# The first microseconds of a four-layer decoder trunk: one DMA queue, tokens and first weights ahead, tap tables later, unread products on TensorE

## Chip, core and metric

One NeuronCore of a Trainium2 chip runs the whole program. The metric is device time in microseconds (us). In the profile PE is TensorE (matmuls and transposes), PEld its weight loads, DVE VectorE, ACT ScalarE, POOL GpSimd and SP SyncE; SPq and ACTq are the DMA queues that SyncE and ScalarE issue on.

## What is computed

The input is 256 tokens of width 1024. Four layers follow; layer i mixes tokens by a gated convolution (i = 0 and 3), a state-space scan (1) or differential attention (2), then attends to 256 memory tokens, then runs a SwiGLU. Each sub-layer ends in a layer norm of alpha * x + f(x). The change touches the start of the program and the convolution:

```python
def conformer_conv(x, w_in, b_in, w_dw, b_dw, ln_g, ln_b, w_out, b_out):
    h = x @ w_in + b_in                      # 1024 -> 2048
    a, gate = jnp.split(h, 2, axis=-1)
    h = a * jax.nn.sigmoid(gate)
    h = causal_depthwise_conv(h, w_dw, b_dw) # 31 taps
    h = jax.nn.silu(layer_norm(h, ln_g, ln_b))
    return h @ w_out + b_out

def reference(x, mem, ...):
    for i in range(4):
        y = (conformer_conv, ssd_mixer, diff_attention)[i % 3](x, ...)
        x = post_norm(x, y, ...)
        x = post_norm(x, memory_cross_attention(x, mem, ...), ...)
        x = post_norm(x, swiglu(x, ...), ...)
    return x
```

## The kernel before

Products of f32 numbers are made of three fp32r matmuls each: a number is split into a rounded high part and the rest (`split`: ScalarE copies the high part, VectorE subtracts), and `mm3` (L199 to L202) adds high x high, high x low and low x high in one PSUM bank.

Weights stream through `_Weights`. A block is 128 x 1024 numbers (512 KB). `_load` (L136 on) takes one of 4 raw buffers, issues the block's DMA (for `cv_w_in` two of 256 KB each, L145), then has ScalarE make the high part `wh` (L152) and VectorE the low part `wl` (L155) in a ring of 7. A raw buffer is free again when its `wl` is made. `get` first calls `prefetch`, which runs `_load` up to AHEAD = 3 blocks past the one wanted.

The tokens are held as two tiles x of 128 rows. `transpose_split` turns a tile on TensorE (L226, four 128x128 transposes into one of two "m" banks), then splits the result into XTh and XTl (L213, L215). The same function turns the memory tokens into MT.

`conv` runs `gated(c)` for four column groups of `w_in`. One `gated` takes four weight blocks and runs `gemm_a`: for t = 0 and 1, for k = 0 to 7, one `mm3` of 512 columns, so 48 matmuls, each block serving two k; after each t, `done` adds the bias (L544), gates (L545, L546), and after every second c splits the result (uh, ul; tiles ch and cl). The convolution is done with a 160-point Fourier transform held as a table `dft`: `front(t, c)` multiplies by the table (6 matmuls for t = 0, 12 for t = 1) and by the spectrum of the taps H on VectorE (L566 to L571), and splits; `rear(t, c)` transforms back (6 matmuls, which need that split). H itself is made in `conv_tables`: 8 f32 matmuls of 31 rows (L502), with a VectorE copy (L503) after each pair's half. Between the gated groups `kv_fill` runs key and value units of the memory attention.

The program order at the start: `conv_loads` (the two small loads ftap and taps on ScalarE's queue, into raw buffers), `setup` (tokens, first weight block, transposes), `conv_tables` (H), then `conv`: gated(0), `conv_dft` (the table, into a raw buffer), both memory tiles, gated(1), ... A planner orders the instructions of each engine by priority (program order, unless `high_priority` raises it) and its own estimate of when each is ready; each engine then runs its list strictly in order. `gemm_a` takes a dict `between`: work to be emitted after a given (t, k), whose TensorE instructions come behind that product (`behind`). Before, gated(2) emits front(0, 0) after (0, 5) and rear(0, 0) and front(1, 0) after (1, 3). Layer 3's convolution uses the same functions, with its loads and tables made during the SwiGLU of layer 2.

Of the kernel before, what the change touches and what calls it, by code (L numbers as in the profile page):

```python
# [9 lines left out]
F32 = mybir.dt.float32  # L10
F32R = mybir.dt.float32r
BF16 = mybir.dt.bfloat16
# [5 lines left out]
P = 128  # L18
# [70 lines left out]

class _FromRaw:  # L90


    def __init__(self, raw):
        self.raw = raw

    def tile(self, shape, dtype, tag, name):
        return self.raw.tile([P, D], dtype, tag="raw", name=name)[0 : shape[0], 0 : shape[1]]

# [11 lines left out]
class _Weights:  # L110
# [3 lines left out]
    def __init__(self, nc, ins, raw_pool, ring_pool, plan):  # L114
        self.nc, self.ins, self.raw_pool, self.ring_pool = nc, ins, raw_pool, ring_pool
        self.plan, self.record = plan, isinstance(nc, _Trace)
        self.pos = self.loaded = 0
        self.ready = {}

    def get(self, name, i, k0, nk, *segs):  # L120
        key = (name, i, k0, nk, segs)
        if self.record:
            self.plan.append(key)
            return self.nc, self.nc
        assert self.plan[self.pos] == key
        self.prefetch(min(len(self.plan), self.pos + 1 + AHEAD))
        wh, wl = self.ready.pop(self.pos)
        self.pos += 1
        return wh, wl
# [5 lines left out]

    def _load(self, q):  # L136
        nc = self.nc
        name, i, k0, nk, segs = self.plan[q]
        n = sum(c for _, c in segs)
        raw = self.raw_pool.tile([P, 1024], F32, tag="raw", name=f"raw{q}")[:, : nk * n]  # L140
        raw3 = raw.rearrange("p (k n) -> p k n", k=nk)
        src = self.ins[name][i]
        at = 0
        for c0, c in segs:
            nc.sync.dma_start(  # L145
                out=raw3[:, :, at : at + c],
                in_=src[k0 * P : (k0 + nk) * P, c0 : c0 + c].rearrange("(k p) n -> p k n", p=P),
            )
            at += c
        wh = self.ring_pool.tile([P, 1024], F32R, tag="wh", name=f"wh{q}")[:, : nk * n]  # L150
        wl = self.ring_pool.tile([P, 1024], F32R, tag="wl", name=f"wl{q}")[:, : nk * n]
        nc.scalar.copy(out=wh, in_=raw)  # L152
        m = nk * n // LO_PARTS
        for a in range(0, nk * n, m):
            nc.vector.tensor_tensor(  # L155
                out=wl[:, a : a + m], in0=raw[:, a : a + m], in1=wh[:, a : a + m].bitcast(F32), op=ALU.subtract
            )
        self.ready[q] = (
            wh.rearrange("p (k n) -> p k n", k=nk),
            wl.rearrange("p (k n) -> p k n", k=nk),  # L160
        )


class _Trunk:
# [45 lines left out]
    def split(self, src, dh, dl, scale=1.0):  # L210

        nc = self.nc
        nc.scalar.activation(out=dh, in_=src, func=AF.Copy, scale=scale)  # L213
        if scale == 1.0:
            nc.vector.tensor_tensor(out=dl, in0=src, in1=dh.bitcast(F32), op=ALU.subtract)  # L215
        else:
            nc.vector.scalar_tensor_tensor(
                out=dl, in0=src, scalar=scale, in1=dh.bitcast(F32), op0=ALU.mult, op1=ALU.subtract
            )

    def transpose_split(self, nat, dh, dl, t, halves=(0, 1)):
        nc = self.nc
        for j in halves:
            ps = self.bank("m", a=4)
            for i in range(4):
                nc.tensor.transpose(ps[:, i, :], nat[:, (4 * j + i) * P : (4 * j + i + 1) * P], self.ident)  # L226
            dst = (slice(None), slice(4 * j, 4 * j + 4), slice(t * P, (t + 1) * P))
            self.split(ps, dh[dst], dl[dst])

# [166 lines left out]

    def setup(self):
        nc, ins = self.nc, self.ins
# [16 lines left out]
        early = self.const.tile([P, 1], F32, name="early")  # L415
        nc.scalar.activation(out=early, in_=self.mhalf[:, 0:1], func=AF.Tanh)
        for t in range(T):
            for c in range(2):
                cs = slice(c * 512, (c + 1) * 512)
                nc.sync.dma_start(out=self.x[t][:, cs], in_=ins["x"][0][t * P : (t + 1) * P, cs])  # L420
            with self.tc.high_priority():
                self.transpose_split(self.x[t], self.XTh, self.XTl, t)
            if t == 0:
                self.W.prefetch(1)

    def load_mem(self):
        for t in range(T):
            m = self.raw.tile([P, D], F32, tag="raw", name=f"mem{t}")
            self.nc.sync.dma_start(out=m, in_=self.ins["mem"][0][t * P : (t + 1) * P, :])
            self.transpose_split(m, self.MTh, self.MTl, t)  # L430

# [52 lines left out]
    def conv_loads(self, pool, tmp, j):  # L484

        nc, ins = self.nc, self.ins
        ftap = tmp.tile([TAPS, 2 * NC], F32, tag="small", name=self.uid("ftap"))
        nc.scalar.dma_start(out=ftap, in_=ins["dft"][0:TAPS, 4 * NC : 6 * NC])
        taps = tmp.tile([TAPS, D], F32, tag="rows", name=self.uid("taps"))
        nc.scalar.dma_start(out=taps, in_=ins["cv_w_dw"][j])  # L490
        return {"raw": (ftap, taps)}

# [12 lines left out]
    def conv_dft(self, pool, tmp, j, pre):  # L505

        nc, ins = self.nc, self.ins
        dft = tmp.tile([P, DFT_COLS], F32, tag="rows", name=self.uid("dft"))
        nc.sync.dma_start(out=dft, in_=ins["dft"])
# [7 lines left out]
    def conv(self, i, j, pre):  # L517
# [5 lines left out]
        with self.stage_pool(f"cv{j}", 1) as pool, self.stage_pool(f"cw{j}", 2) as wk:  # L523
# [9 lines left out]
            def gated(c, between={}):  # L533
# [19 lines left out]

                self.gemm_a("cv_w_in", j, ((c * 256, 256), (D + c * 256, 256)), done, "i", between)

# [19 lines left out]
            def rear(t, c):  # L575
                self.mm3(nat[t][c], *back[0], *ysp, True, False)
                self.mm3(nat[t][c], *back[1], *psp, False, True)
                nc.vector.bn_stats(out=st[t][:, c, :], in_=nat[t][c])

            gated(0)  # L580
            if "late" in pre:
                pre.pop("late")()
            dfts, H, yre = pre["dft"], pre["H"], pre["yre"]
            now = [[d[:, q * NC : (q + 1) * NC] for d in dfts] for q in range(2)]
# [3 lines left out]
            psp = [pool.tile([NF, 512], F32R, name=f"cv_z{e}") for e in "hl"]  # L588
            if first:
                self.load_mem()  # L590
            gated(1)
            bo = self.bcast_row("raw", ins["cv_b_out"][j], self.raw)
            for t in range(T):
# [32 lines left out]
            fill = KV_CONV[j]  # L626
            gated(2, {(0, 5): lambda: front(0, 0), (1, 3): lambda: (rear(0, 0), front(1, 0))})
            self.kv_fill(i, fill[0])
# [767 lines left out]
    def run(self):  # L1396
        n = 0
        ctx = ExitStack()
        pre, (loads, tables, late) = self.prepare(0, ctx, _FromRaw(self.raw))
        loads()  # L1400
        self.setup()
        tables()
        pre["late"] = late
        for i in range(DEPTH):
# [67 lines left out]
```

## Time and profile before

| | us |
|---|---|
| median of 3 runs (lowest, highest) | 1749.15 (1746.3, 1751.69) |
| the profiled execution, its own time | 1747.02 |
| its span from first to last instruction | 1745.3 |

TensorE is busy 98% of the span. The first of the 40 slices of the page (43.6 us each) is the one in which it is least busy, with 6 tenths. Times below are microseconds from the start of the span unless marked ns. A start and a duration stand first in a timeline row; a bracket at its end says how long the engine was idle before it and what ended that. A pipelined matmul's duration overlaps the next one's, so the pace of a run of matmuls is read from start to start. "PEclk" in a table of stretches is the granted clock as a share of full speed (2.4 GHz; 0.5 is 1.2 GHz).

### The profile page before, as it was taken

To read this page: it belongs to the slowest core of one execution; us is meant where nothing else is said; L and a number is where in the kernel's file an instruction comes from. 1 tells how busy PE (TensorE), PEld (TensorE's weight loads), DVE (VectorE), ACT (ScalarE), POOL (GpSimd) and SP (SyncE) were. 2 spreads that over 40 slices of the span, in tenths; PEclk is the share of its full clock that TensorE was granted. 3 is DMA by queue.
4 is the path that set the end of the run, shared out by engine and by line. 5 is a ranking of instruction groups with operands and counts; after the bars stand their busy time and mean duration, and the time that the engine had idled before them with its cause. 6 is when DMAs were issued, how large, how long until landed. Compare 5 with 4: busy or idle time off the path is not lost.

```text
span 1745.3 us, 25786 instructions
## 1 busy us (share of the span) xinstructions
PE 1704.7 (98%) x9788; PEld 1470.4 (84%) x9788; DVE 1283.2 (74%) x1965; ACT 905.4 (52%) x1436; POOL 67.8 (4%) x72
## 2 busy tenths in 40 slices
PE   6999999999999999999999999999999999999998
PEld 4898888888999998888888888888788878878886
DVE  4898776668898778776668677776666888876666
ACT  3455555554665654455554565545454445645552
POOL 0000000000011110000000000000000000000000
PEclk9999999999999999999999999999999999999999
DMA  6656376666666545376665643647566645556662
GB/s 227 218 169 202 117 217 186 188 191 181 193 182 173 181 146 191 115 219 192 192 186 190 180 133 109 193 143 216 161 192 194 211 151 167 184 168 189 187 191 73
DMA packets 234084, 309.84 MB, mean 178 GB/s; under 512 B 14104, under 2 KB 196774, under 8 KB 233960
## 3 DMA queue, kind: packets, MB, share of 16 engines
q1 hardware_dynamic: 233832, 307.90, 57.0%
q8 instruction: 77, 1.26, 0.3%
q14 instruction: 47, 0.39, 0.1%
q10 hardware_dynamic: 128, 0.29, 0.0%
HBM read 307.07 MB, written 1.08 MB: 177 GB/s over the span
## 4 chain that ended last, share of the span: by engine, by line
PE 76%; DVE 7%; DMA 4%; ACT 2%; issue 2%; POOL 0%; SPq 0%; DVEq 0%; ACTq 0%; POOLq 0%
PE psi L284 20%; PE psi L286 10%; PE pso L332 6%; PE pso L333 6%; PE pso L336 6%; PE psi L202 4%; PE psi L200 4%; PE psi L201 4%; PE pso L200 4%; PE pso L201 4%; PE pso L202 4%; DVE wl L155 2%; DMA raw<-in_xa_w_out 1%; ACT wh L152 1%; DMA raw<-in_ff_w_in 1%
## 5 line engine op out<-in xcount | busy, mean ns | idle before, releaser
L155 DVE TENSOR_TENSOR wl<-raw,wh 128x1024 fp32r<-128x1024 f32 x537 | 653.8, 1221 | 284.3 <-ACT wh L152 279.6
L152 ACT CAST wh<-raw 128x1024 fp32r<-128x1024 f32 x537 | 561.1, 1050 | 481.1 <-issue 120.9
L284 PE MATMUL psi<-XT,wh 128*128 128x512 f32 x1408 | 386.8, 396 | 2.7 <-DVE xnat L302 1.6
L284 PEld LDWEIGHTS psi<-XT,wh 128*128 128x128 f32 x1408 | 243.9, 189 | 39.0 <-PE psm L202 2.3
L286 PEld LDWEIGHTS psi<-XT,wl 128*128 128x128 f32 x1408 | 216.3, 189 | 31.0 <-issue 1.6
L286 PE MATMUL psi<-XT,wl 128*128 128x256 f32 x1408 | 224.9, 281 | 0.0
L332 PE MATMUL pso<-wh,ch 128*128 128x512 f32 x448 | 176.6, 394 | 0.0
L333 PE MATMUL pso<-wl,ch 128*128 128x512 f32 x448 | 175.2, 391 | 0.0
L336 PE MATMUL pso<-wh,cl 128*128 128x512 f32 x448 | 139.6, 391 | 0.0
L200 PE MATMUL psi<-XT,wh 128*128 128x256 f32 x384 | 109.7, 286 | 1.1 <-DVE zz L956 1.1
L202 PE MATMUL psi<-XT,wl 128*128 128x256 f32 x384 | 109.9, 286 | 0.0
L201 PE MATMUL psi<-XT,wh 128*128 128x256 f32 x384 | 108.8, 283 | 0.0
L241 POOL TENSOR_TENSOR rs<-rv,mhalf 128x1 f32<-128x1 f32 (+2 forms) x40 | 48.5, 1212 | 1339.7 <-DVE rv L240 1326.8
L336 PEld LDWEIGHTS pso<-wh,cl 128*128 128x128 f32 x448 | 84.0, 188 | 17.8
L333 PEld LDWEIGHTS pso<-wl,ch 128*128 128x128 f32 x448 | 84.2, 188 | 16.1
L332 PEld LDWEIGHTS pso<-wh,ch 128*128 128x128 f32 x448 | 84.2, 188 | 15.6
L200 PE MATMUL pso<-wh,XT 128*128 128x512 f32 x224 | 89.9, 401 | 0.6 <-ACT XT L213 0.5
L202 PE MATMUL pso<-wh,XT 128*128 128x512 f32 x224 | 88.3, 394 | 0.3 <-DVE XT L215 0.3
L201 PE MATMUL pso<-wl,XT 128*128 128x512 f32 x224 | 87.8, 392 | 0.0
L200 PE MATMUL pso<-wh,ch 128*128 128x512 f32 x192 | 76.0, 396 | 0.0
L200 PEld LDWEIGHTS psi<-XT,wh 128*128 128x128 f32 x384 | 73.6, 192 | 2.0 <-issue 1.6
L201 PE MATMUL pso<-wl,ch 128*128 128x512 f32 x192 | 75.0, 391 | 0.0
(331 smaller groups left out, 2987.2 us busy)
## 6 DMA issues: line engine op xcount, KB each, us to landing
raw<-in_ff_w_in SPq DMA_DIRECT2D x160, 512.0 KB, 4.7
raw<-in_ff_w_out SPq DMA_DIRECT2D x88, 512.0 KB, 4.2
raw<-in_xa_w_kv SPq DMA_DIRECT2D x64, 512.0 KB, 4.7
raw<-in_cv_w_in SPq DMA_DIRECT2D x64, 256.0 KB, 5.4
raw<-in_xa_w_q SPq DMA_DIRECT2D x32, 512.0 KB, 4.4
raw<-in_xa_w_out SPq DMA_DIRECT2D x32, 512.0 KB, 4.6
raw<-in_mb_w_in SPq DMA_DIRECT2D x32, 512.0 KB, 4.8
raw<-in_da_w_qkv SPq DMA_DIRECT2D x24, 512.0 KB, 4.5
```

The source lines that it names most:

```text
L152: nc.scalar.copy(out=wh, in_=raw)
L155: nc.vector.tensor_tensor(out=wl[:, a : a + m], in0=raw[:, a : a + m], in1=wh[:, a : a + m].bitcast(F32), op=ALU.subtract)
L200: mm(out, ah, bh, start=start, stop=False)
L201: mm(out, ah, bl, start=False, stop=False)
L202: self.last_mm = mm(out, al, bh, start=False, stop=stop)
L241: nc.gpsimd.tensor_tensor(out=r, in0=v, in1=self.mhalf[:, :cols], op=ALU.pow)
L284: mm(ps, wh[:, k, js], X[:, 4 * b + k, :], start=b == 0 and k == 0, stop=False)
L286: self.last_mm = mm(ps[:, S : 2 * S], wl[:, k, js], X[:, 4 * b + k, 0:S], start=False, stop=b == 1 and k == 3)
L332: mm(acc[t][c], hh[:, ts], wh[:, 0, cs], start=first, stop=False)
L333: mm(acc[t][c], hh[:, ts], wl[:, 0, cs], start=False, stop=False)
L336: mm(acc[t][c], hl[:, ts], wh[:, 0, cs], start=False, stop=last)
```

## The change

- Loads at the start all go on SyncE's queue: the first token tile, weight blocks 0 to 2, the second token tile, block 3, then ftap (now 32 rows) and the taps, as two transfers of 16 rows (rows 0 to 15 and 15 to 30). `_load` is parted into `fetch` (buffer and DMA) and the casts.
- ftap, taps and dft no longer take raw buffers; they lie in memK, which is not written until the first key unit (`_Lent`).
- ScalarE's first two weight casts are put behind the last copy of the first token tile (`issue_after`). During gated(0) nothing is cast past the block wanted (`ahead` = 0); after it, four more blocks are fetched and two cast, behind the last copy of the second token tile.
- The second token tile is turned after (0, 5) of gated(0). The memory tiles are turned after (0, 5) and (1, 1) of gated(1), their loads behind the weights fetched by then; H is made after (1, 7) of gated(1).
- front(0, 0) is emitted after (0, 1) of gated(2) in place of (0, 5), in both convolution layers.
- `warm(n)` issues n bf16 matmuls of 512 columns on a constant tile, whose results nothing reads: 6 at the very start, 7 behind the transposes of the first token tile.

```diff
@@ class _Lent (for _FromRaw) @@
     def tile(self, shape, dtype, tag, name):
-        return self.raw.tile([P, D], dtype, tag="raw", name=name)[0 : shape[0], 0 : shape[1]]
+        at = {"rows": 0, "small": D, "wide": D + 256}[tag]
+        return self.t.rearrange("p a b -> p (a b)")[0 : shape[0], at : at + shape[1]]
@@ class _Weights @@
-        self.prefetch(min(len(self.plan), self.pos + 1 + AHEAD))
+        self.prefetch(min(len(self.plan), self.pos + 1 + self.ahead))
...
+    def fetch(self, n):
+        while not self.record and self.fetched < n:
+            self._fetch(self.fetched)
+            self.fetched += 1
...
+    def _load(self, q):
+        self.fetch(q + 1)
+        nc, raw = self.nc, self.arriving.pop(q)
@@ setup @@
+    def warm(self, n):
+        if not hasattr(self, "any"):
+            self.any = self.chunk.tile([P, 512], BF16, tag="cl", name="any")
+            self.nc.vector.memset(self.any, 1.0)
+        ps = self.bank("o")
+        for _ in range(n):
+            self.nc.tensor.matmul(ps, self.any[:, 0:P], self.any, start=True, stop=True)
...
+        self.warm(6)
         for t in range(T):
             for c in range(2):
                 cs = slice(c * 512, (c + 1) * 512)
                 nc.sync.dma_start(out=self.x[t][:, cs], in_=ins["x"][0][t * P : (t + 1) * P, cs])
-            with self.tc.high_priority():
-                self.transpose_split(self.x[t], self.XTh, self.XTl, t)
             if t == 0:
-                self.W.prefetch(1)
...
+                self.W.fetch(3)
+        self.W.fetch(4)
+        ahead()
+        with self.tc.high_priority():
+            last = self.transpose_split(self.x[0], self.XTh, self.XTl, 0)
+        with self.tc.issue_after(self.last_transpose.ins):
+            self.warm(7)
+        with self.tc.issue_after(last.ins):
+            self.W.prefetch(2)
+
+    def load_mem(self, t):
+        m = self.raw.tile([P, D], F32, tag="raw", name=f"mem{t}")
+        self.nc.sync.dma_start(out=m, in_=self.ins["mem"][0][t * P : (t + 1) * P, :])
+        self.transpose_split(m, self.MTh, self.MTl, t)
@@ conv_loads @@
-        ftap = tmp.tile([TAPS, 2 * NC], F32, tag="small", name=self.uid("ftap"))
-        nc.scalar.dma_start(out=ftap, in_=ins["dft"][0:TAPS, 4 * NC : 6 * NC])
+        ftap = tmp.tile([32, 2 * NC], F32, tag="small", name=self.uid("ftap"))
+        nc.sync.dma_start(out=ftap, in_=ins["dft"][0:32, 4 * NC : 6 * NC])
         taps = tmp.tile([TAPS, D], F32, tag="rows", name=self.uid("taps"))
-        nc.scalar.dma_start(out=taps, in_=ins["cv_w_dw"][j])
-        return {"raw": (ftap, taps)}
+
+        for k in (0, TAPS - 16):
+            nc.sync.dma_start(out=taps[k : k + 16], in_=ins["cv_w_dw"][j][k : k + 16])
+        return {"raw": (ftap[0:TAPS], taps)}
@@ conv @@
+            if first:
+                self.W.ahead = 0
             gated(0)
+            if first:
+                self.W.ahead = AHEAD
+                self.W.fetch(2 * RAW)
+                with self.tc.issue_after(self.last_copy.ins):
+                    self.W.prefetch(RAW + 2)
+                pre["between"] = {
+                    (0, 5): lambda: self.load_mem(0), (1, 1): lambda: self.load_mem(1), (1, 7): pre.pop("tables"),
+                }
...
-            if first:
-                self.load_mem()
             gated(1)
+            H = pre["H"]
...
-            gated(2, {(0, 5): lambda: front(0, 0), (1, 3): lambda: (rear(0, 0), front(1, 0))})
+            gated(2, {(0, 1): lambda: front(0, 0), (1, 3): lambda: (rear(0, 0), front(1, 0))})
@@ run @@
-        pre, (loads, tables, late) = self.prepare(0, ctx, _FromRaw(self.raw))
-        loads()
-        self.setup()
-        tables()
-        pre["late"] = late
+        def ahead():
+            steps.extend(self.prepare(0, ctx, _Lent(self.memK)))
+            steps[1][0]()
+
+        self.setup(ahead)
+        pre, (_, tables, pre["late"]) = steps
...
+        def second():
+            self.last_copy = self.transpose_split(self.x[1], self.XTh, self.XTl, 1)
+
+        pre["between"] = {(0, 5): second}
+        pre["tables"] = tables
```

## Rows read from the trace of the kernel before

**Rows 1.** The waits of TensorE over the whole run: engine, line, what it waited for, then us in total, times, longest.

```profile
PE psm L226 <- DMA x<-in_x: 7.0, 2, 4.7
PE psi L200 <- ACT XT L213: 4.9, 1, 4.9
PE pso L200 <- ACT cv_yh L213: 3.6, 2, 2.1
```

**Rows 2.** The timeline of the start, all engines.

```profile
0.80 0.85 SPq L420 DMA_DIRECT2D x<-in_x  x2
...
1.71 1.19 SPq L145 DMA_DIRECT2D raw<-in_cv_w_in  x2
...
4.71 1.09 PE L226 MATMUL psm<-ident,x 128*128 128x128 f32 x4 [4.71 <-DMA x<-in_x]
...
8.07 1.11 PE L226 MATMUL psm<-ident,x 128*128 128x128 f32 x4 [2.27 <-DMA x<-in_x]
11.73 0.89 SPq L145 DMA_DIRECT2D raw<-in_cv_w_in  x2
12.44 1.04 ACT L152 CAST wh<-raw 128x1024 fp32r<-128x1024 f32 x1 [9.36 <-DMA raw<-in_cv_w_in]
13.39 0.59 ACT L213 ACTIVATE XT<-psm 128x512 fp32r<-128x512 f32 x1
13.52 1.23 DVE L155 TENSOR_TENSOR wl<-raw,wh 128x1024 fp32r<-128x1024 f32 x1 [12.44 <-ACT wh L152]
...
14.03 0.79 PE L200 MATMUL psi<-wh,XT 128*128 128x512 f32 x1 [4.85 <-ACT XT L213]
...
15.91 1.04 ACT L152 CAST wh<-raw 128x1024 fp32r<-128x1024 f32 x1 [1.93 <-DMA raw<-in_cv_w_in]
```

**Rows 3.** The waits of SyncE's queue in the first 20 us, columns as in Rows 1.

```profile
SPq L145 <- DMA taps<-in_cv_w_dw: 6.0, 1, 6.0
```

**Rows 4.** Stretches of 3 us from the start: length, then busy us of PE, PEld, DVE, ACT and POOL, then granted clock, busy share of the DMA engines, GB/s moved.

```profile
3.00:6.00 3.00, 1.09 (x4) 0.71 (x4) 0.00 (x0) 0.08 (x1) 0.00 (x0) 1.00 0.92 306
...
9.00:12.00 3.00, 0.18 (x1) 0.00 (x0) 0.00 (x0) 0.00 (x0) 0.00 (x0) 1.00 0.07 25
```

**Rows 5.** TensorE's timeline from 14 to 36 us: gated(0), the H matmuls, the first memory transposes.

```profile
17.16 0.63 PE L201 MATMUL psi<-wl,XT 128*128 128x512 f32 x1
17.59 0.63 PE L202 MATMUL psi<-wh,XT 128*128 128x512 f32 x1
...
19.29 0.48 PE L202 MATMUL psi<-wh,XT 128*128 128x512 f32 x1
...
20.07 0.40 PE L202 MATMUL psi<-wh,XT 128*128 128x512 f32 x1
20.30 0.39 PE L200 MATMUL psi<-wh,XT 128*128 128x512 f32 x1
...
21.37 3.80 PE L502 MATMUL psm<-taps,ftap 31*82 31x512 f32 x8
...
25.67 0.62 PE L201 MATMUL psi<-wl,XT 128*128 128x512 f32 x1
...
28.64 0.60 PE L202 MATMUL psi<-wh,XT 128*128 128x512 f32 x1
...
35.23 0.93 PE L226 MATMUL psm<-ident,mem 128*128 128x128 f32 x7
```

**Rows 6.** Stretches of 2 us after the H matmuls of layer 0 and after those of layer 3 (made near 1245 us), columns as in Rows 4.

```profile
26.00:28.00 2.00, 2.00 (x6) 1.53 (x5) 0.88 (x3) 1.04 (x1) 0.00 (x0) 0.50 0.96 352
...
1248.00:1250.00 2.00, 2.00 (x6) 1.27 (x6) 0.92 (x2) 0.00 (x0) 0.00 (x0) 0.50 0.41 117
```

**Rows 7.** The timeline of gated(1): the two places in which TensorE waited in it.

```profile
41.31 0.50 PE L200 MATMUL psi<-wh,XT 128*128 128x512 f32 x1 [0.60 <-ACT wh L152]
...
42.57 0.50 PE L201 MATMUL psi<-wl,XT 128*128 128x512 f32 x1 [0.76 <-DVE wl L155]
```

**Rows 8.** The timeline of gated(2) in layer 0, from its first front matmul to the first product of the memory keys behind it.

```profile
53.39 0.39 PE L200 MATMUL psm<-ch,cv_dft0h 128*82 128x512 f32 x1
...
57.87 0.68 DVE L566 TENSOR_TENSOR cvp<-psm,cv_H 81x512 f32<-81x512 f32 x1
...
63.04 0.50 PE L200 MATMUL pso<-cv_yh,cv_dft0h 82*128 82x512 f32 x1 [1.46 <-ACT cv_yh L213]
...
68.11 0.28 PE L200 MATMUL psi<-MT,wh 128*128 128x256 f32 x1
```

**Rows 9.** The stretch of 5 us between the first two of them, columns as in Rows 4.

```profile
50.00:55.00 5.00, 5.00 (x24) 3.90 (x23) 5.00 (x8) 3.95 (x5) 0.00 (x0) 1.00 0.81 260
```

**Rows 10.** The timeline of gated(2) in layer 3, up to its first rear matmul.

```profile
1387.29 0.39 PE L200 MATMUL psi<-wh,XT 128*128 128x512 f32 x1
...
1388.46 0.69 DVE L215 TENSOR_TENSOR cl<-cv_u,ch 128x512 fp32r<-128x512 f32 x1
...
1391.37 0.39 PE L200 MATMUL psm<-ch,cv_dft1h 128*82 128x512 f32 x1
```

**Rows 11.** The same timeline onward, from the first rear matmul.

```profile
1399.59 0.50 PE L200 MATMUL pso<-cv_yh,cv_dft1h 82*128 82x512 f32 x1 [2.14 <-ACT cv_yh L213]
...
1401.35 0.63 PE L200 MATMUL pso<-cv_zh,cv_dft1h 81*128 81x512 f32 x1
...
1404.34 0.54 PE L200 MATMUL psm<-ch,cv_dft1h 128*82 128x512 f32 x1
```

More of the change, by code (lines that the diff above doesn't have):

```diff
@@ L87, in __exit__, with __init__ @@
         return False
-class _FromRaw:
-    def __init__(self, raw):
-        self.raw = raw
+class _Lent:
+    def __init__(self, t):
+        self.t = t
     def tile(self, shape, dtype, tag, name):
-        return self.raw.tile([P, D], dtype, tag="raw", name=name)[0 : shape[0], 0 : shape[1]]
+        at = {"rows": 0, "small": D, "wide": D + 256}[tag]
+        return self.t.rearrange("p a b -> p (a b)")[0 : shape[0], at : at + shape[1]]
 class _Late:
@@ L116, in __init__ @@
         self.plan, self.record = plan, isinstance(nc, _Trace)
-        self.pos = self.loaded = 0
-        self.ready = {}
+        self.pos = self.loaded = self.fetched = 0
+        self.arriving, self.ready = {}, {}
+        self.ahead = AHEAD
     def get(self, name, i, k0, nk, *segs):
@@ L134, in prefetch, with _fetch @@
             self.loaded += 1
-    def _load(self, q):
+    def fetch(self, n):
+        while not self.record and self.fetched < n:
+            self._fetch(self.fetched)
+            self.fetched += 1
+    def _fetch(self, q):
         nc = self.nc
@@ L149, in _load @@
             at += c
+        self.arriving[q] = raw
+    def _load(self, q):
+        self.fetch(q + 1)
+        nc, raw = self.nc, self.arriving.pop(q)
+        _, _, _, nk, segs = self.plan[q]
+        n = sum(c for _, c in segs)
         wh = self.ring_pool.tile([P, 1024], F32R, tag="wh", name=f"wh{q}")[:, : nk * n]
@@ L212, in split @@
         nc = self.nc
-        nc.scalar.activation(out=dh, in_=src, func=AF.Copy, scale=scale)
+        first = nc.scalar.activation(out=dh, in_=src, func=AF.Copy, scale=scale)
         if scale == 1.0:
@@ L219, in split @@
             )
+        return first
     def transpose_split(self, nat, dh, dl, t, halves=(0, 1)):
@@ L225, in transpose_split @@
             for i in range(4):
-                nc.tensor.transpose(ps[:, i, :], nat[:, (4 * j + i) * P : (4 * j + i + 1) * P], self.ident)
+                self.last_transpose = nc.tensor.transpose(ps[:, i, :], nat[:, (4 * j + i) * P : (4 * j + i + 1) * P], self.ident)
             dst = (slice(None), slice(4 * j, 4 * j + 4), slice(t * P, (t + 1) * P))
-            self.split(ps, dh[dst], dl[dst])
+            last = self.split(ps, dh[dst], dl[dst])
+        return last
     def bcast_row(self, tag, row, pool=None, n=D):
@@ L394, in post_norm, with setup @@
                     self.transpose_split(x, self.XTh, self.XTl, t, halves=(c,))
-    def setup(self):
+    def warm(self, n):
[5 more added lines that the diff above has]
+            self.nc.tensor.matmul(ps, self.any[:, 0:P], self.any, start=True, stop=True)
+    def setup(self, ahead):
         nc, ins = self.nc, self.ins
@@ L420, in setup @@
                 nc.sync.dma_start(out=self.x[t][:, cs], in_=ins["x"][0][t * P : (t + 1) * P, cs])
-            with self.tc.high_priority():
-                self.transpose_split(self.x[t], self.XTh, self.XTl, t)
             if t == 0:
-                self.W.prefetch(1)
[L426 to L430, printed above, removed]
+                self.W.fetch(3)
[11 more added lines that the diff above has]
+        self.transpose_split(m, self.MTh, self.MTl, t)
     def kv_steps(self, layer):
@@ L507, in conv_dft @@
         nc, ins = self.nc, self.ins
-        dft = tmp.tile([P, DFT_COLS], F32, tag="rows", name=self.uid("dft"))
+        dft = tmp.tile([P, DFT_COLS], F32, tag="wide", name=self.uid("dft"))
         nc.sync.dma_start(out=dft, in_=ins["dft"])
@@ L552, in done @@
                         self.split(us[t][:, 256 * c - 256 : 256 * c + 256], uh[t][c // 2], ul[t][c // 2])
-                self.gemm_a("cv_w_in", j, ((c * 256, 256), (D + c * 256, 256)), done, "i", between)
+                self.gemm_a(
+                    "cv_w_in", j, ((c * 256, 256), (D + c * 256, 256)), done, "i", between or pre.pop("between", {})
+                )
             def front(t, c):
@@ L578, in rear @@
                 nc.vector.bn_stats(out=st[t][:, c, :], in_=nat[t][c])
+            if first:
+                self.W.ahead = 0
             gated(0)
+            if first:
[6 more added lines that the diff above has]
+                }
             if "late" in pre:
                 pre.pop("late")()
-            dfts, H, yre = pre["dft"], pre["H"], pre["yre"]
+            dfts, yre = pre["dft"], pre["yre"]
             now = [[d[:, q * NC : (q + 1) * NC] for d in dfts] for q in range(2)]
@@ L1398, in run @@
         ctx = ExitStack()
[L1399 to L1403 removed]
+        steps = []
+        def ahead():
[7 more added lines that the diff above has]
+        pre["tables"] = tables
         for i in range(DEPTH):
```

## The prediction

> **What bounds the kernel now.** I read the waits of TensorE over the whole run first. Of the long ones, the two longest stand at the very start: 7.0 us for the tokens and 4.9 us for their split copy; then come 3.6 us in two waits of the convolution's rear matmuls, one in layer 0 and one in layer 3 [rows 1]. All other time is matmuls in a row, so a beginning that ends earlier ends the program earlier by as much, if what follows keeps its order. The question is how much earlier, and what the moved work costs where it goes.
>
> The timeline of the start shows the chain. The first half of the first token tile is turned at 4.71, the second at 8.07, though both loads are issued in the first microsecond or so. The first weight block, issued at 1.71, is cast at 12.44; ScalarE copies the turned tokens only behind that cast (13.39), and the first product runs at 14.03 [rows 2]. SyncE meanwhile waits 6.0 us for the taps before it issues the second block [rows 3]. From 3 to 6 us the DMA engines move 306 GB/s, from 9 to 12 us 25 GB/s [rows 4]: the weight block does not wait for bandwidth, it waits with one slow transfer, the 31 rows of taps. That is the load the change splits, and moves behind.
>
> The products run start to start in 0.43 us until 19.29 and in 0.23 us after it [rows 5]. These are the paces of TensorE's two levels, 1.2 and 2.4 GHz: from 26 to 28 us, where the granted clock is recorded as 0.50 [rows 6], the pace is 0.42 [rows 5]. Ahead of 19.29 the record shows no fall, and only the pace tells the level.
>
> **The start, step by step.** *Tokens.* A 512 KB pair of transfers that finds the engines idle is cast 4.2 us after its first issue (11.73 to 15.91 [rows 2]), so tokens issued at 0.80 are there at about 5.0. Each 512 KB behind them takes 0.524 MB / 306 GB/s = 1.7 us [rows 4]: block 0 at 6.7, block 1 at 8.4, block 2 at 10.1, the second token tile at 11.8, block 3 at 13.5. SyncE issues a pair in 0.85 to 1.19 us [rows 2], less than the pair's transfer, so the single queue does not hold the data up.
>
> *First product.* Second half turned 5.0 + 1.1 = 6.1; copied by ScalarE 6.7 (0.59); block 0 cast 7.8 (1.04, now behind the copy), its low part 9.0 (1.23) [rows 2]. Blocks 1 and 2 follow at the pace of the loads, and VectorE's 1.23 per block is under 1.7. Block 3: 13.5 + 1.04 + 1.23 = 15.8. The second tile is turned in the gap before block 3, so turning it costs TensorE nothing there. From 15.8 some five products of block 3 (1.2) and 24 products of the second tile (24 x 0.23 = 5.5) are left: gated(0) ends at 22.5. Before it ended at 35.2 with the H matmuls inside it [rows 5]. **Gain 12.7.** Bounds: at the 352 GB/s of a later stretch [rows 6] the blocks come every 1.5 us and the end is at 21.5; with block 3 or the second tile's split a cast later (1.04 + 1.23), 24.8.
>
> *Unread products.* The nearest rows, 512 columns in 0.23 to 0.43 us [rows 5], put six at 1.4 to 2.6 us, between about 1.3 and 4, done before the tokens land; seven take 1.6 to 3.0 from 6.1, so they end by 9.1, when block 0's low part is ready. Cost 0 to 0.4, taken as 0. Their gain is the pace of the next products. If they do not raise the clock, it rises 5.3 us after the first product as before (14.03 to 19.29 [rows 2, 5]), and blocks 0 and 1 run at 0.43; as they wait for loads anyway, I work out only 0.7 us of delay at the end of block 3.
>
> *Taps.* They go behind 12 issues on SyncE's queue and ahead of block 4. Nothing needs them until H. The trace shows no 16-row transfer: between the pace of 25 GB/s [rows 4] (131 KB: 5.2 us) and 306 GB/s (0.4 us), block 4, due at 22.5, would be late by nothing or by at most some 2 us, so I take 0. Rule against row: the Trainium skill, "DMA: Bandwidth & Descriptors", section "Why a DMA increments its semaphore by 16 and not by 1", says that 31 rows run on one DMA engine and 16 rows on 16; by it the two transfers are short and the sum stays as it is, by the slow row it loses up to 2. The same skill's "Trainium Kernel Development and Optimization", section "Key Constraints", speaks against part of the change: queues share the same engines, and issuing from several saves issue time, which a single queue gives up. By it three issues of some 0.43 us are added on SyncE; in the rows they cost nothing, since SyncE, done with all of them near 7 us, waits for the first free raw buffer (block 0's low part, 9.0) in any case.
>
> **What is paid back later.** *H.* Eight matmuls in 3.8 us [rows 5] now follow gated(1) and no longer stand in gated(0): **minus 3.8**, up to minus 5 if they wait for VectorE's copies. Behind them the clock falls: 0.50 after those of layer 0 and of layer 3 alike [rows 6], and from 25.67 to 28.64 seven products take 2.97 us [rows 5] where 7 x 0.23 = 1.6 is their fast pace: **minus 1.4** (0 if the denser surroundings keep the clock).
>
> *Memory tiles.* Their transposes cost the same in gated(1). But their loads stand behind the weights. After block 3: taps 0.15 MB, blocks 4 to 7 2.1, dft 0.4, two bias pairs 0.5, blocks 8 to 10 1.6, the first memory tile 0.5: 5.25 MB / 306 GB/s = 17.2 us, so 30.7; at 352 GB/s 14.9 from 12.8, so 27.7. TensorE wants it after 18 products of gated(1), 22.5 + 4.1 = 26.6. Waits of 1.1 to 4.1 us; the planner may put the transposes behind further products instead, which makes it 0. Queued behind a waiting transpose is all of TensorE's list. **Minus 2**, range 0 to minus 5.
>
> *Weights of gated(1).* The two waits there, 0.60 and 0.76 [rows 7], were for a late block. Blocks 4 to 7 now land some 4 us or more before their products: **plus 1.4**, at worst 0.
>
> *front(0, 0) four k earlier,* 4 x 3 x 0.23 = 2.7 us. In layer 0 rear waits 1.46 [rows 8], because VectorE, full from 50 to 55 us [rows 9], begins front's chain only at 57.87, 4.5 us after front's first matmul at 53.39 [rows 8]. It stays nearly full, with H's four copies added and H's matmul time too: **plus 1.2**, from plus 1.5 to minus 1.5. In layer 3 rear waits 2.14, and then seven matmuls from 1401.35 to 1404.34 run at the slow pace [rows 11], another 1.4: together 3.5. There front would come at 1387.29 + 6 x 0.23 = 1388.7 in place of 1391.37, and its operand cl is done at 1388.46 + 0.69 = 1389.2 [rows 10]: it waits 0.5 at most and ends 2.2 earlier. **Plus 2.5**, from minus 0.5 to plus 3.5.
>
> **Sum.** 12.7 - 3.8 - 1.4 - 2 + 1.4 + 1.2 + 2.5 = 10.6 us. The profiled execution took 1747.0, 2.1 under the median of 1749.15, and the three runs spread over 5.4; I take the middle of these two, 1748.1, and get **1737.5**. All best ends give 13.7 - 3.8 + 1.4 + 1.5 + 3.5 = 16.3 (1731.8), all worst 10.4 - 5 - 1.4 - 5 - 1.5 - 0.5 = -3.0 (1751.1).
>
> **Rivals.** *More:* the planner moves the memory transposes out of the way and TensorE keeps its clock behind H: 2 + 1.4 and 1.3 more from the two rear waits, 15.3 in all, 1733. For it: the planner already mixes transposes among products before. Against: the clock fell behind H both times [rows 6].
>
> *The gain is taken back by VectorE and the loads:* the memory tile is 5 us late, the clock falls in that wait as it does behind the 2.14 us wait [rows 11] (1.4), and the earlier front brings nothing, because VectorE stays full [rows 9] (3.7): 10.6 - 3 - 1.4 - 3.7 = 2.5, 1745.6, no measurable change.
>
> *Slower:* the queue before the memory tiles also carries the three 512 KB rows that were issued early before (two norm rows and the output bias: 1.6 MB, 5.1 us). Then the first memory tile comes 9.2 us late, the second 1.7 us after it, each followed by 1.4 of slow clock: 13.7 in place of 2, a sum of -1.1, 1749 and upward. It turns to a loss when these waits and what follows them pass 12.6 us. Against it: those rows have no use until after gated(3).
>
> *It does not do what it says:* the unread products leave the clock low (0.7) or the split taps stay slow (up to 2): 1738 to 1740.
>
> **How the numbers follow.** Forecast 0.57 at 1737.5, not what it says 0.09, more 0.14, taken back 0.15, slower 0.05. A measurement of this kernel can tell about 0.3%, 5.2 us, from no change. The first three cases lie below 1743.9: faster 0.80, within 0.3% 0.15, slower 0.05. The range from 1731 to 1744 holds those three cases and leaves out the other two.
>
> **What would show it.** Right: no wait of SyncE for taps; the first weight cast behind the first token copies at 6 to 8 us; the first real product near 8 to 9 at a pace of 0.23; gated(0) over between 21.5 and 24.8; the H matmuls near 36 to 42 with a stretch of clock 0.50 behind them; the first key product of layer 0 some 8 us earlier than 68.11 [rows 8]; the rear wait of layer 3 gone. Wrong: a transfer that lands much later than 1.7 us per 512 KB, a wait of TensorE of over 5 us on a memory tile, or a longer chain on VectorE before the first rear.

## The result, and the profile after

| | before | after |
|---|---|---|
| median, us (runs; lowest, highest) | 1747.72 (4; 1744.41, 1751.69) | 1736.12 (4; 1734.43, 1737.21) |
| ratio with 95% interval | | 0.994 (0.9918 to 0.9962) |
| profiled execution, its own time | 1747.02 | 1736.67 |
| its span | 1745.3 | 1734.9 |

Faster by 0.6%, and the forecast (1737.5, from 1731 to 1744) holds. The profiled executions differ by 10.35 us, the medians by 11.6 here and by 8.8 in a second group of runs on another chip (e9); the sum was 10.6. The waits of TensorE over the whole run, as in [rows 1]; columns: us in total, times, longest:

```profile
PE pso L421 <- DVE any L418: 1.7, 1, 1.7
...
PE psi L215 <- ACT wh L167: 1.3, 1, 1.3
...
PE psm L216 <- DVE cl L230: 0.9, 1, 0.9
...
PE psi L216 <- DVE wl L170: 0.8, 1, 0.8
...
PE pso L215 <- ACT cv_yh L228: 0.2, 1, 0.2
...
PE psm L242 <- DMA mem<-in_mem: 0.2, 1, 0.2
```

The 7.0 us for tokens and the 4.9 for their copy are off the list, in part only because the unread products fill the time: without them TensorE waits 3.7 us for the tokens and 3.3 for the first weight block (e3). What was gained is read from the first product, below. The 3.6 at the rear matmuls are 0.2 for cv_yh, the operand that they waited for. The first row is the wait of the unread products for their constant tile, which delays nothing. The timeline of the start, all engines, answers to [rows 2]:

```profile
1.68 2.74 PE L421 MATMUL pso<-any 128*128 128x512 bf16 x6 [1.68 <-DVE any L418]
1.71 3.00 SPq L153 DMA_DIRECT2D raw<-in_cv_w_in  x6
...
4.21 1.91 PE L242 MATMUL psm<-ident,x 128*128 128x128 f32 x8
...
5.92 2.29 PE L421 MATMUL pso<-any 128*128 128x512 bf16 x7
...
8.46 1.04 ACT L167 CAST wh<-raw 128x1024 fp32r<-128x1024 f32 x1 [1.70 <-DMA raw<-in_cv_w_in]
...
9.53 1.23 DVE L170 TENSOR_TENSOR wl<-raw,wh 128x1024 fp32r<-128x1024 f32 x1 [2.05 <-ACT wh L167]
9.55 0.50 PE L215 MATMUL psi<-wh,XT 128*128 128x512 f32 x1 [1.34 <-ACT wh L167]
...
9.91 1.04 ACT L167 CAST wh<-raw 128x1024 fp32r<-128x1024 f32 x1 [0.41 <-DMA raw<-in_cv_w_in]
...
14.60 1.05 ACT L167 CAST wh<-raw 128x1024 fp32r<-128x1024 f32 x1 [2.15 <-DMA raw<-in_cv_w_in]
```

Tokens are turned at 4.21, the first weight block is cast at 8.46 in place of 12.44, and the first product runs at 9.55 in place of 14.03. The forecast had block 0 cast by 7.8. The stretches of 3 us, columns as in [rows 4], show how much had been moved by then:

```profile
0.00:3.00 3.00, 1.32 (x4) 0.49 (x5) 0.67 (x3) 1.49 (x2) 0.50 (x5) 1.00 0.32 97
3.00:6.00 3.00, 3.00 (x13) 2.17 (x12) 0.06 (x1) 0.60 (x1) 0.00 (x0) 1.00 0.87 258
6.00:9.00 3.00, 2.21 (x8) 0.65 (x6) 1.32 (x2) 1.14 (x2) 0.00 (x0) 1.00 1.01 342
9.00:12.00 3.00, 1.69 (x4) 1.18 (x5) 2.24 (x2) 2.14 (x3) 0.00 (x0) 0.76 1.05 364
```

None of them is down at the 25 GB/s of 9 to 12 us before: the slow transfer is gone from there. But by 8.46 us 0.29 + 0.77 + 0.84 = 1.9 MB have moved, where the first token tile and block 0 are 1.05. So loads queued behind block 0 had moved some 0.85 MB by the time it was there. Blocks 1 and 2 are cast 1.45 and 1.50 us behind it, at 9.91 and 11.41, one after another at the forecast pace (1.5 to 1.7); block 3, forecast to land at 13.5, is cast at 14.60. The later part of layer 0, TensorE's timeline:

```profile
23.97 0.39 PE L215 MATMUL psi<-wh,XT 128*128 128x512 f32 x1
...
33.17 1.07 PE L242 MATMUL psm<-ident,mem 128*128 128x128 f32 x8 [0.20 <-DMA mem<-in_mem]
...
39.25 1.94 PE L536 MATMUL psm<-memK 31*82 31x512 f32 x4 [0.20 <-DVE MT L230]
41.12 0.50 PE L217 MATMUL psi<-wh,XT 128*128 128x512 f32 x1
41.55 1.08 PE L536 MATMUL psm<-memK 31*82 31x512 f32 x2
42.56 0.50 PE L215 MATMUL psi<-wh,XT 128*128 128x512 f32 x1
42.99 1.08 PE L536 MATMUL psm<-memK 31*82 31x512 f32 x2
44.01 0.50 PE L216 MATMUL psi<-wl,XT 128*128 128x512 f32 x1
...
55.55 0.50 PE L215 MATMUL pso<-cv_yh,cv_dft0h 82*128 82x512 f32 x1 [0.23 <-ACT cv_yh L228]
...
60.17 0.28 PE L215 MATMUL psi<-MT,wh 128*128 128x256 f32 x1
```

The row at 23.97 is the first product of gated(1) (the 49th of the layer; I counted them); in the profile before the 49th starts at 34.55. The planner put the memory transposes at 33.17, behind more products than I had assumed, so they wait 0.2 us. The H matmuls stand in three pieces between products. The first key product, 68.11 in [rows 8], is at 60.17: 7.94 earlier. Lastly the waits of TensorE from 1375 to 1405 us, gated(2) of layer 3, where [rows 11] had one of 2.14 and a slow stretch behind it:

```profile
PE psm L216 <- DVE cl L230: 0.9, 1, 0.9
PE pso L215 <- ACT cv_zh L228: 0.5, 1, 0.5
PE pso L216 <- DVE cv_zl L230: 0.3, 1, 0.3
PE psm L215 <- ACT ch L228: 0.3, 1, 0.3
PE pso L216 <- DVE cv_yl L230: 0.2, 1, 0.2
```

The one long wait has become five short ones, 2.2 us in all; what is gone is the slow stretch. In the seven other executions with the earlier front three or four waits are left here, 0.9 to 1.8 us in all.

### The profile page after: what moved, and what is told of

It is laid out like the page before. It is cut to its first block, busy times and chain, and to the rows that moved or that the text cites. A ratio compares the mean times of both kernels' runs of the same rounds, so it can differ in the third digit from the quotient of the medians.

```text
span 1734.9 us, 25812 instructions
## 1 busy us (share of the span) xinstructions
PE 1706.1 (98%) x9801; PEld 1470.1 (85%) x9801; DVE 1284.5 (74%) x1966; ACT 906.3 (52%) x1436; POOL 67.9 (4%) x72
## 3 DMA queue, kind: packets, MB, share of 16 engines
HBM read 307.08 MB, written 1.08 MB: 178 GB/s over the span
```

## Experiments

I followed each run by its **lag**: the start of a product in the profile before less the start of the same product (by its place in TensorE's list) in the run, so the us gained up to there. "Layer 0" is its median over 70 to 150 us, "end" over 1580 to 1700. A **fall** is a stretch in which the trace records a granted clock of 0.50, 1.2 GHz; (L) marks those of 6.8 us, the others last 3.4. The fall behind the last product is left out. In the profile before they begin at 25.7, 1247.6 (L) and 1401.2.

| run | median us (runs) | ratio to before (95%) | layer 0 | end | falls begin at |
|---|---|---|---|---|---|
| after | 1736.12 (4) | 0.994 (0.9918 to 0.9962) | 7.9 | 10.5 | 10.6, 1239.4 (L) |
| e1 | 1738.59 (10) | 0.9973 (0.9962 to 0.9984) | 6.5 | 8.2 | 424.0, 1393.4 |
| e2 | 1742.01 (10) | 0.9992 (0.9982 to 1.0002) | 1.8 | 3.3 | 34.9, 45.2 (L), 485.5, 1553.9 |
| e3 | 1737.2 (4) | 0.9958 (0.9942 to 0.9974) | 7.5 | 10.8 | 43.5, 422.4, 951.5 |
| e4 | 1736.36 (4) | 0.9952 (0.9935 to 0.9968) | 9.4 | 9.9 | 41.9, 420.8, 1240.0 (L), 1547.2 |
| e5 | 1740.11 (8) | 0.9974 (0.9957 to 0.9991) | 7.4 | 12.3 | 29.3, 1544.8 |
| e6 | 1732.75 (5) | 0.9937 (0.9916 to 0.9958) | 9.5 | 16.9 | none |
| e7 | 1736.04 (6) | 0.9951 (0.9936 to 0.9966) | 4.6 | 12.3 | 11.6, 42.3 (L), 424.6 |
| e8 | 1738.13 (10) | 0.9969 (0.9953 to 0.9985) | 6.0 | 8.6 | 43.4 (L), 1391.7, 1548.7 |
| e9 | 1736.76 (6) | 0.995 (0.9934 to 0.9967) | 6.0 | 10.9 | 42.8 (L) |
| e10 | 1733.05 (4) | 0.9926 (0.9913 to 0.9938) | 8.7 | 13.5 | 420.7, 1543.7 |
| e11 | 1737.54 (6) | 0.9955 (0.994 to 0.997) | 7.7 | 8.6 | 39.3 (L), 1240.8 (L), 1394.4 |
| e12 | 1737.0 (6) | 0.9944 (0.9929 to 0.9958) | 8.5 | 5.0 | 11.7, 421.3, 479.3, 953.8, 1394.1 (L) |

e1 to e4 ran on one chip, e5 to e8 on a second, e9 to e12 on a third, each group beside the kernel before (1743.27, 1743.56 and 1745.57). The lag is that of one execution.

**e1: the kernel before, with the loads of ftap and taps changed alone:** ftap has 32 rows in place of 31, and the taps come in two transfers.

```diff
-        ftap = tmp.tile([TAPS, 2 * NC], F32, ...)
-        nc.scalar.dma_start(out=ftap, in_=ins["dft"][0:TAPS, ...])
+        ftap = tmp.tile([32, 2 * NC], F32, ...)
+        nc.scalar.dma_start(out=ftap, in_=ins["dft"][0:32, ...])
-        nc.scalar.dma_start(out=taps, in_=ins["cv_w_dw"][j])
+        for k in (0, TAPS - 16):
+            nc.scalar.dma_start(out=taps[k : k + 16], in_=ins["cv_w_dw"][j][k : k + 16])
```

> The kernel before with one part of the change alone: ftap as 32 rows, the taps as two transfers of 16 rows, still on ScalarE's queue. Theory (the 31-row transfer holds back the start): SyncE's wait of 6.0 us for the taps goes, the first weight cast moves from 12.44 to about 8, the first product from 14.03 to about 10, and 4 to 5 us of the total go. Rival (the order of the loads is what counts, the slow transfer only looks guilty): the first cast stays past 11 and less than 1 us goes.

TensorE's waits up to 70 us, and two rows of the timeline:

```profile
PE psm L226 <- DMA x<-in_x: 4.0, 1, 4.0
PE psi L200 <- ACT XT L213: 2.3, 1, 2.3
```

```profile
6.92 1.04 ACT L152 CAST wh<-raw 128x1024 fp32r<-128x1024 f32 x1 [3.70 <-DMA raw<-in_cv_w_in]
...
8.51 0.80 PE L200 MATMUL psi<-wh,XT 128*128 128x512 f32 x1 [2.34 <-ACT XT L213]
```

The waits are 4.0 and 2.3 against 7.0 and 4.9 in [rows 1]. From 6 to 9 us the DMA engines move 327 GB/s. The first block is cast at 6.92, where the rival (the order counts) had it past 11, and the first product runs at 8.51, a microsecond earlier than in the changed kernel's profile. Three lines, without a new order, give 0.27%, about half of the whole gain of 0.5 to 0.6%. The lag in layer 0 is 6.5, but some 1.4 of it is the slow stretch behind H [rows 6], which this execution did not have. The 31 rows of ftap were not tried alone; in e2 ftap has 32.

**e2: the changed kernel, taps in one transfer of 31 rows**, still behind block 3.

```diff
-        for k in (0, TAPS - 16):
-            nc.sync.dma_start(out=taps[k : k + 16], in_=ins["cv_w_dw"][j][k : k + 16])
+        nc.sync.dma_start(out=taps, in_=ins["cv_w_dw"][j])
```

> The changed kernel with the taps as one transfer of 31 rows again, in their new place behind block 3. Theory (the place is enough, since nothing that is wanted soon stands behind them): blocks 4 and 5 land up to 5 us later, which their slack covers; total 0 to 1.5 us above the changed kernel. Rival (the split is needed wherever the taps stand): TensorE waits for block 4 or 5 near 24 us, total 4 to 6 us above.

A stretch of 2 us, columns as in [rows 4], and two rows of the timeline:

```profile
17.00:19.00 2.00, 2.00 (x11) 1.63 (x10) 0.69 (x2) 0.00 (x0) 0.00 (x0) 1.00 0.34 113
```

```profile
20.80 1.05 ACT L167 CAST wh<-raw 128x1024 fp32r<-128x1024 f32 x1 [4.33 <-DMA raw<-in_cv_w_in]
...
35.13 1.94 PE L242 MATMUL psm<-ident,mem 128*128 128x128 f32 x8 [2.85 <-DMA mem<-in_mem]
```

Nothing that is clear of noise is left of the gain (1742.01 beside 1743.27). gated(0) ends as early as in the changed kernel. Then the loads behind the slow transfer are late: ScalarE waits 4.33 us for a block, TensorE 2.85 for a memory tile, and the clock falls once in that wait and once behind H. So the split is needed even where nothing waits for the taps themselves. The 31 rows hold up what is queued behind them, the two transfers of 16 rows do not. The rule of the Trainium skill that the prediction weighed ("DMA: Bandwidth & Descriptors", "Why a DMA increments its semaphore by 16 and not by 1"), one DMA engine for 31 rows and 16 for 16 rows, agrees with the trace of before: from 9 to 12 us the busy share of the 16 engines is 0.07 [rows 4], about one engine.

**e3: no unread products** (both calls of `warm` removed), and **e7: 14 in place of the 7 behind the transposes**. Nothing reads what they add or omit.

```diff
-        self.warm(6)
...
-        with self.tc.issue_after(self.last_transpose.ins):
-            self.warm(7)
```

> The changed kernel without the unread products (both groups; no result depends on them). Theory (they only raise the clock early, and the first blocks wait for loads anyway): the first real products run at 0.43 us until about 15, the first key product comes 0.5 to 1.5 us later than 60.17. Rival 1 (they are worth nothing, because the granted clock falls at 10.87 us all the same): less than 0.3 us. Rival 2 (they carry the start): 3 us or more.

```diff
-            self.warm(7)
+            self.warm(14)
```

> The changed kernel with 14 unread products in place of 7 behind the first transposes, so that TensorE is not idle from 8.2 to 9.55. Theory (the idle stretch before the first real product lets the clock fall at 10.87, and seven products then run at 0.43): the fall goes, the first key product comes 1.0 to 1.5 us earlier than 60.17, total 1 to 1.5 us below. Rival 1 (the pace of the first blocks is set by their loads): under 0.4 us. Rival 2 (seven more products delay the first real one): 0 to 1 us above.

All intervals overlap with that of the same kernel with 7 (e9). Without them the first products do run at the pace of 1.2 GHz: from 10.82 to 12.10 three products take 1.28 us in e3; in e9, with them, three take 0.69 from 10.85. Yet the 24th product starts at 17.6 in e3 and at 17.7 in e9, since both wait for the loads. And in the profile of the changed kernel the clock fell at 10.6, during the first real products: in that execution the six and seven unread products did not keep it up, nor did the fourteen in e7 (a fall at 11.6). In eight of the eleven executions with unread products no fall came there.

**e4 and e8: front(0, 0) after (0, 5), as before, and after (0, 3).**

```diff
-            gated(2, {(0, 1): lambda: front(0, 0), ...
+            gated(2, {(0, 5): lambda: front(0, 0), ...
```

> The changed kernel with front(0, 0) back after (0, 5). Theory (the earlier front removes rear's wait): rear waits again about 1.5 us in layer 0 and 2 us in layer 3, there with the clock fallen behind it; total 1.5 to 3.5 us above the changed kernel. Rival (VectorE is full, the front's place matters little): under 0.7 us.

> The changed kernel with front(0, 0) after (0, 3). Theory (in layer 3 front now waits 0.25 and 0.87 us for its own operand, and this place removes that and keeps rear's wait short): layer 3 gains 0.5 to 1.1 us, layer 0 keeps its place, total 0.3 to 1 us below the changed kernel. Rival (what front no longer waits, rear waits again): within 0.3 us of the changed kernel or above.

In layer 0 the earlier front brings nothing: e4, with the old place, has no rear wait there either and the larger lag, 9.4; e1, also with the old place, has one of 0.3. In layer 3 e4 waits 2.3 us at the rear as before, but with no fall behind it. Over all traces: with front after (0, 1) none of eight executions has a fall between 1390 and 1402; after (0, 5) or (0, 3) five of six have one (before, e1, e8, e11, e12, not e4). Around 1400 the lag grows by 1.1 to 2.3 in seven of the eight (0.4 in the changed kernel's own profile); e4, with the old place and no fall, grows by 1.5 as well. So it is the fall that costs; that the place of front decides whether it comes rests on these counts. With front after (0, 3), e8, rear waits 1.0 us, the clock falls at 1391.7, and the median is not below that of the changed kernel. The medians of e4 and of the changed kernel can't be told apart.

**e5: H in gated(0) after (1, 7)**, the rest as changed.

```diff
-                    (0, 5): ..., (1, 1): ..., (1, 7): pre.pop("tables"),
+                    (0, 5): ..., (1, 1): ...,
...
-        pre["between"] = {(0, 5): second}
+        pre["between"] = {(0, 5): second, (1, 7): tables}
```

> The changed kernel with the H matmuls behind (1, 7) of gated(0) in place of (1, 7) of gated(1). Theory (H costs TensorE the same 3.7 to 4.3 us in either place, and only the clock behind it can differ): the clock falls behind H as in the kernel before, 1 to 1.5 us lost, total 0.5 to 2 us above the changed kernel. Rival (moving H back is itself worth what it costs, since it waits for VectorE's copies and the products wait with it): total 0.5 us or more below the changed kernel.

1740.11, slower than its neighbour e7 by 4. Its profile is of its fastest run (1734.86), so the trace can't say where; the runs above 1739 have mean granted clocks of 0.993 to 0.995, the three below 0.996 to 0.997. The intervals of e5 and e7 overlap, so it is likely, and not shown, that moving H behind gated(1) pays through the clock; I had it only as a cost.

**e6: both memory tiles before gated(1)**, as in the kernel before.

```diff
+            if first:
+                self.load_mem(0)
+                self.load_mem(1)
             gated(1)
```

> The changed kernel with both memory tiles asked for before gated(1) in the program order, as before. Theory (the planner puts the transposes where it expects the tile, so the emitted place decides little): TensorE's wait on a memory tile stays under 1 us, total within 1 us of the changed kernel. Rival (the later place is what avoids the wait, the transposes stand in TensorE's list ahead of products): a wait of 2 to 5 us near 24 to 30, total 2 to 5 us above.

The wait for the tile is 0.5 us, and the profile is the only one without a fall; it has the largest lag of all, 16.9. But it is of the fastest of the five runs (1730.23). The interval still overlaps with that of the changed kernel. One of the five, 1738.17, is listed with a mean granted clock of 0.944, far lower than its time would lead one to expect; why is open.

**e9: the changed kernel again.**

> The changed kernel itself, a second time, so that its falls of the clock can be compared between two executions of one program. Theory (where the clock falls differs from execution to execution, and the difference between the variants so far is mostly that): the instructions before a fall lie where they lay, but the list of falls is another one; the first key product moves by 1.5 us for each fall of 3.4 us more or fewer ahead of it and by 3.1 us for one of 6.8. Rival (the falls belong to the program): the same falls as before, at 10.9 and near 1240, and 60.2 for the first key product within 0.3 us.

Two stretches of 2 us, one behind H in layer 0 and one at H in layer 3; PEclk is the third number from the end. First e9, then the execution shown above:

```profile
44.00:46.00 2.00, 2.00 (x4) 1.10 (x4) 1.18 (x2) 1.08 (x2) 0.00 (x0) 0.50 1.08 351
1240.00:1242.00 2.00, 2.00 (x5) 0.63 (x6) 1.23 (x3) 1.04 (x1) 0.00 (x0) 1.00 0.59 179
```

```profile
44.00:46.00 2.00, 2.00 (x10) 1.45 (x10) 1.29 (x2) 1.05 (x1) 0.00 (x0) 1.00 1.10 353
1240.00:1242.00 2.00, 2.00 (x4) 0.35 (x2) 0.00 (x0) 0.00 (x0) 0.00 (x0) 0.50 0.65 240
```

One program, two executions: one falls behind the first H, the other behind the second. From the end of gated(1) to the keys the lag goes from 12.1 to 6.0 in e9 and from 11.6 to 7.9 in the other, so the fall behind the first H cost 12.1 - 6.0 - (11.6 - 7.9) = 2.4 us; not having the one before at 1247.6 gives e9 3.1. Over e9's six runs the time follows the mean granted clock: 1733.57 at 0.998, 1743.13 at 0.992. So 10 us lie between runs of one program, as much as the change moves, and a lag that a single profile shows must first be freed of its falls.

**e10: H from 128 rows**, the rows past the 31 taps filled with zeros, so that H is unchanged.

```diff
-        ftap = tmp.tile([32, 2 * NC], F32, ...)
+        ftap = tmp.tile([P, 2 * NC], F32, ...)
-        taps = tmp.tile([TAPS, D], F32, ...)
+        taps = tmp.tile([P, D], F32, ...)
+        nc.gpsimd.memset(taps, 0.0)
```

> The changed kernel with the H matmuls on 128 rows, the added ones zero (ftap loaded with all 128 rows, the taps tile set to zero by GpSimd first), same columns. Theory (what makes the clock fall behind H is matmuls on 31 rows): no fall within 10 us behind H in either convolution layer, H's own time the same within 0.3 us; the total 1 to 3 us below the changed kernel. Rival (the rows do not matter, the f32 matmuls with their pauses do): falls near 43 or 1240 as in most runs so far.

TensorE's timeline at H:

```profile
38.30 1.95 PE L537 MATMUL psm<-memK 128*82 128x512 f32 x4 [0.72 <-DVE MT L230]
...
40.31 1.02 PE L537 MATMUL psm<-memK 128*82 128x512 f32 x2
```

Four times the rows cost no time (1.95 and 1.02 beside 1.94 and 1.08), and in this execution no fall follows H in either layer. With 31 rows and H in one place (not spread as in e12), nine of twelve executions fell around H in layer 0 and four of thirteen in layer 3. The four runs have mean clocks of 0.997 to 0.999 and times from 1731.78 to 1733.71; e9's six, on the same chip, 0.992 to 0.998 and 1733.57 to 1743.13. It is the best ratio of all, though its interval still touches e9's (0.9934).

**e11: memory tiles early, front after (0, 5), taps as 16 and 15 rows**, and **e12: that with H's four pairs spread over gated(1).**

```diff
-        for k in (0, TAPS - 16):
-            nc.sync.dma_start(out=taps[k : k + 16], in_=ins["cv_w_dw"][j][k : k + 16])
+        for k, n in ((0, 16), (16, 15)):
+            nc.sync.dma_start(out=taps[k : k + n], in_=ins["cv_w_dw"][j][k : k + n])
```

> The changed kernel with three edits together: both memory tiles asked for before gated(1), front(0, 0) back after (0, 5), and the taps as rows 0 to 15 and 16 to 30, which do not overlap. Theory (each of the first two gave 1 to 1.5 us in layer 0 once falls of the clock are taken out; the overlap makes SyncE wait 2.4 us for the first transfer, which nothing on TensorE's path needs): first key product 1.5 to 3 us earlier than 60.17 without a fall, total 1 to 3 us below the changed kernel. Rival (the two gains are one, or were falls): within 1 us of it.

```diff
-                    (1, 7): pre.pop("tables"),
+                    (n // 2, 3 + 4 * (n % 2)): lambda n=n: pre["tables"](n) for n in range(4)
```

> As e11, with the four pairs of H matmuls of layer 0 behind (0, 3), (0, 7), (1, 3) and (1, 7) of gated(1) in place of all behind (1, 7). Theory (products between the H matmuls keep the clock up, and VectorE's copies are hidden by them): no fall behind H in layer 0, no wait on a copy of H, first key product 0.5 to 2 us earlier than in e11. Rival (H costs its 3.7 us wherever it stands): within 0.3 us of e11, if e11 has no fall there.

Neither beats e6 or e10. In both the rear of layer 3 waits again (2.2 and 2.5 us) and the clock falls at it, where e4 had no fall. Of the 8.3 us of lag between e6 and e11, e11's three falls make some 6.9 (2.4 and 3.1 as in e9, 1.4 as in the prediction). Without overlapping halves SyncE's queue no longer waits for the first (2.4 us in the changed kernel), with no gain to be seen. Spreading H kept the clock around it, in one execution. Padding H together with the early memory tiles wasn't tried.

## Why the prediction was right, point by point

- **The slow transfer of taps bounds the start: shown.** Its split, with one row more for ftap, gives about half of the gain (e1). Left in one piece in the new place it no longer bounds the start, but the loads behind it, and the other edits then give nothing (e2). "Taps: 0" held. Its sign, no wait of SyncE for taps, did not: SyncE waits 2.4 us for the first of the two transfers, and nothing on TensorE's path needed it.
- **gated(0) ends 12.7 earlier: right in mechanism, 2.1 too large.** Product 49 moved from 34.55 to 23.97, 10.6. I had taken the old end 0.7 too late (35.23 is a transpose behind three products of gated(1)) and the new one 1.5 too early. The mis-sized term is the landing of the weights: 1.7 us for each 512 KB in order gave 6.7 for block 0 and 13.5 for block 3; they were cast at 8.46 and 14.60. The end hangs on block 3, as the forecast had it. In e9, without a fall at the start, TensorE waits for its low part, and product 49 follows at 23.39:

```profile
16.69 0.50 PE L216 MATMUL psi<-wl,XT 128*128 128x512 f32 x1 [0.70 <-DVE wl L170]
```

In e11 block 0 is cast already at 6.50 but block 3 at 14.24, and product 49 starts at 23.31. In the changed kernel's own profile the fall at 10.6, with products at 0.43 us, adds some 0.3. So two signs were missed: the first cast (6 to 8) and the first product (8 to 9, at a pace of 0.23). Nor was SyncE done with these issues near 7 us: it issued the first part of the taps at 9.85.

- **Memory tiles -2, weights of gated(1) +1.4:** together +1.0 in place of -0.6. The planner took the transposes out of the way (wait 0.2), the case that I had given 0. (In that term 12.8 should read 12.5, five blocks of 1.5 us behind 5.0; it moves only the lower bound of the wait, from 1.1 to 0.8.)
- **H -3.8 and the clock behind it -1.4:** 4.7 in the profile, from the end of the last product ahead (38.66 + 0.23) to 44.01, less the two products between (0.46). It did not fall behind H in this execution; in e9 it did, for 2.4 more. The forecast of 5.2 lies between the two. Whether the clock falls behind H differs between executions of this one program.
- **Unread products 0: held,** and the rival's 0.7 for a low clock is not there either, because the loads set the end (e3).
- **Earlier front, layer 0 +1.2: size right, reason wrong.** From the end of H to the first key product 1.0 was gained, but the rear wait goes without the earlier front too (e4). What removes it wasn't isolated.
- **Earlier front, layer 3 +2.5: too large,** 0.4 in the profile, 1.1 to 2.3 in seven other executions. The wait does not go, it is cut into five, of 2.2 us in all (0.9 to 1.8 in the others); what goes is the fall behind it, which e4 lacks too. I had said that front would wait 0.5 for cl; it waited 0.9, with four further waits.
- **The sum:** layer 0 gave 10.6 + 1.0 - 4.7 + 1.0 = 7.9 (forecast 8.1), layer 3 0.4 (2.5), and 2.1 came from places that the forecast did not name. What held is that a beginning which ends earlier ends the program earlier by as much: from the keys to 1390 us the lag stays at about 8 to 9. So the total of 10.46 is nearer to 10.6 than the terms deserve: that part is luck. Of the 2.1, three waits of the kernel before are parts, here from its whole run:

```profile
PE psm L668 <- ACT xnat L665: 2.0, 2, 1.6
...
PE psm L777 <- DVE fh L774: 1.2, 1, 1.2
PE psi L284 <- DVE fga L302: 1.1, 1, 1.1
```

After, the second and third are gone and the first is 0.6 at its longest, though 1.5 again in e9. The third is at most 0.3 in all other traces looked at for it (e1, e3, e4, e6, e9, e10), e1's included, whose code there is that of before. Why it is gone is open; a profile of before in a second execution would tell.

Open too: whether e6's order or the padding of H is worth its 3 us in the median, or only met with fewer falls. Their own runs speak for the padding. The single queue, the tables in memK and the place of the first casts were not tried apart, so which of them makes the other half of the gain is open as well.

## What to carry to other kernels

Where a stretch at the start moves 25 GB/s, look for one small transfer like these 31 rows, split it before anything else is laid out anew, and find out how much of the gain that is alone. Put a price on a removed wait only after asking what else is late by then: here it came back in five pieces. And profile the unchanged program twice before reading a microsecond out of one trace.

## What the hardware showed that was not expected

- Of three loads issued in a row on one queue (casts at 8.46, 9.91 and 11.41 us) the first landed only after 1.9 MB had moved, 0.85 more than it and the tokens ahead of it; in e11 the first was cast at 6.50 and the second at 9.42. The landing of the first doesn't follow from its own bytes and those ahead of it.
- The granted clock falls at different places in executions of one program (42.8 us in e9; 10.6 and 1239.4 in the other), and with it the time varies by up to 10 us. A like wait need not bring a like fall: near 421 us TensorE waits 1.8 us in the changed kernel's profile without one, and 1.7 in e10 with one (420.7).
- f32 matmuls of 128 rows take as long as those of 31 (1.95 us beside 1.94 for four), and behind the two groups of 128 rows traced the clock stayed at 2.4 GHz.
- Unread products just ahead did not always hold the clock: in the changed kernel's profile it was 0.50 from 10.6 us on, 0.76 on the mean of 9 to 12 us, after TensorE had waited 1.34 us for its first product and 0.76 for its second; in eight of eleven executions with them it stayed up there.
